# Sixty-four bytes of padding ahead of each pool that holds a token sum

## The chip, the core and the metric

The kernel runs on one core of a Trainium2 chip. The metric is the device time of one execution in microseconds (us); a shorter time is better. Several executions are timed, and their median stands for a kernel.

## The reference

One inference step of a small streaming encoder: 1024 new frames ("prompt") and 8 streams of 16 frames ("sample", 128 rows), a model width of 1024, two layers. Each layer is attention followed by an MLP with a hidden width of 4096:

```python
def mlp(x, g_norm, w_up, w_down):
    return jnp.square(jax.nn.relu(rmsnorm(x, g_norm) @ w_up)) @ w_down
...
    for layer in range(DEPTH):
        ...                      # attention; hp (prompt), hs (sample) updated
        hp = hp + mlp(hp, g_mlp[layer], w_up[layer], w_down[layer])
        hs = hs + mlp(hs, g_mlp[layer], w_up[layer], w_down[layer])
```

Everything is float32. This study is about the first MLP product, `rmsnorm(x) @ w_up`, and the change-over from it to the second.

## The kernel before, in words

A layer goes through four stages: `attention`, `wo_phase` (output projection, norm, transposes), `mlp_up` (first MLP product, relu, square) and `mlp_down` (second product).

**Arithmetic.** A float32 operand is split into a rounded part and a remainder (`split`, L106: ScalarE's CAST writes the rounded part at L109, VectorE's TENSOR_TENSOR the remainder at L115). A product of two split operands is three TensorE matmuls (`mm3`, L713: lines L715, L716 and L717). In a matmul row of the profile the names behind the arrow are the moving operand and then the stationary one, so `ps_x<-sx,w` streams 512 tokens of `sx` past 128 columns of `w`. Each matmul has its own weight load (PEld).

**mlp_up.** The product is a Strassen-like scheme with seven products instead of eight. The prompt's tokens are combined to seven "token sums", each a pair of tiles `sx` (rounded part and remainder, 8192 bytes a partition each) in a pool of its own, `h0` to `h6`; `h7` holds the sample's tokens `x8` (two tiles of 4096 bytes). `up_pools` (L727) opens these eight pools on the right side of the on-chip memory (SBUF) in the order 6, 2, 3, 5, 7, 4, 1, 0; the right side grows downwards, so each later pool lies lower. Below them come `uq` (the weight tiles `wq` of the upper half) and `ur` (three buffers `ru` for raw weights). The other weight tiles `w` and the activations `hc`, `hs` are on the left side.

The hidden width is walked in 16 blocks. A block is the seven products of 12 matmuls each, in the order X0, Z1, X5, then the sample (24 matmuls with 256 moving columns, `ps_s`), X6, Y4, the sample's two transposes (`turn`, L807), X3, Y2. The letter is the PSUM bank (`ps_x`, `ps_y`, `ps_z`), the number the product; product p streams token sum SIDE[p], which is sums 0, 1, 4, (sample), 5, 3, 2, 6 in this order. X and Y are added to, so between two products on a bank its content must be read out:

```python
product(X, 6, False, True)
a = nc.scalar.copy(v[3], X)          # L843
product(Y, 4, True, True)
b = tt(v[3], Y, v[3], ALU.add)       # L845
act(v[3], v[3])                      # L788, L789
product(X, 3, False, True)
act(v[2], X)
product(Y, 2, False, True)
tt(v[1], Y, v[1], ALU.add)           # L854
```

Block 0 is done in two halves of 256 tokens; the other fifteen stream all 512.

**mlp_down.** Its tiles are placed over those of `mlp_up`. On the right, `w2` lies where `h2` was, `s2` where `h3` was, `r5` and `r6` where `h5`, `h8` where `h7`, `s1` where `h4`, `w1` where `h1`, `s0` where `h0`. On the left, `r0` and then the residual tiles `x` follow each other upwards over the last activations, `ur` and `uq`. Before the change the borders of the two layouts coincide. The first product of `mlp_down` needs `w0` (split of `r0`) and `s0`; the second needs `w1` (split of `r1`) and `s1`.

**What sets the order.** One queue per engine, in the order in which a scheduler (a timeline simulation at build time) laid the instructions. A DMA issued by SyncE (SP) waits, in its queue, until the tiles whose place it overwrites have been read; everything behind it on SP waits with it. The first loads of `mlp_down` (`load`, L937, shown at line L938) are chained in program order and given a raised priority.

Of the kernel before, what the change touches and what calls it, by code (L numbers as in the profile page):

```python
# [75 lines left out]
class Build:  # L76
# [650 lines left out]
    def up_pools(self, st, layer):  # L727
        sx = [None] * 8
        for p in (6, 2, 3, 5, 7, 4, 1, 0):
            pool = self.pool(st, f"h{p}_{layer}", side="right")  # L730
            shape = [P, KC, P] if p == 7 else [P, 4, NT // 2 * P]
            sx[p] = [pool.tile(shape, F32R, tag=f"sx{v}", name="sx") for v in range(2)]
        qp = self.pool(st, f"uq{layer}", side="right")
        rp = self.pool(st, f"ur{layer}", side="right")
        return sx[:7], sx[7], (qp, rp)
# [1063 lines left out]
```

## Time and profile before

| what | value |
|---|---|
| median of 3 runs | 2407.91 us (2406.41 to 2412.36) |
| span of the profiled execution | 2399.3 us, 8.6 us under that median |
| TensorE busy | 2320.4 us, 97% of the span |
| ScalarE / VectorE busy | 1217.9 us (51%) / 1626.3 us (68%) |
| DMA moved | 385.88 MB, 161 GB/s in the mean |

The profile tells of one execution; its time is known by its span alone. A busy TensorE is not one at its peak: matmuls overlap, so what a matmul costs in a dense stretch is the distance from its start to the next one's start, not its listed length.

### The profile page before, as it was taken

How to read it: one execution, taken by the hardware profiler on the slowest of the kernel's cores; microseconds unless marked ns; L12 is line 12 of the kernel's file. 1: busy time of each engine (PE TensorE's matmuls, PEld its weight loads, DVE VectorE, ACT ScalarE, POOL GpSimd, SP SyncE). 2: the span in 40 equal slices, each digit the busy share in tenths (PEclk: the TensorE clock that was granted, in tenths of full speed). 3: DMA queues.
4: the chain of work that ended last, by engine and by line, in shares of the span. 5: the costliest groups of instructions: out<-in, count | busy, mean ns of one | idle time of the engine just before them, and what ended most of it. 6: DMA issues, size and time to landing. Idle time of an engine off the chain costs nothing.

```text
span 2399.3 us, 33421 instructions
## 1 busy us (share of the span) xinstructions
PE 2320.4 (97%) x11621; PEld 1935.5 (81%) x11621; DVE 1626.3 (68%) x3002; ACT 1217.9 (51%) x2423; POOL 535.6 (22%) x828
## 2 busy tenths in 40 slices
PE   7998999899999999999999999998999999999999
PEld 6786877788888888888777788887888888888887
DVE  6687786755655777776567877877655555776674
ACT  4676675555555433232267666665655555333321
POOL 3343332312112100000333434344211211000000
PEclk9998999999999999999999999999999999999999
DMA  7345546244433874342743555555434435744332
GB/s 244 122 127 168 171 156 200 95 155 158 145 128 141 323 245 146 117 141 99 237 149 111 188 161 173 173 169 174 138 127 145 154 137 200 278 140 158 112 116 114
DMA packets 218457, 385.88 MB, mean 161 GB/s; under 512 B 50408, under 2 KB 125104, under 8 KB 211120
## 3 DMA queue, kind: packets, MB, share of 16 engines
q1 hardware_dynamic: 195136, 307.16, 39.0%
q0 software_dynamic: 21776, 71.84, 7.7%
q10 hardware_dynamic: 1376, 4.74, 0.5%
q8 instruction: 92, 1.51, 0.3%
q14 instruction: 77, 0.63, 0.1%
HBM read 246.47 MB, written 136.14 MB: 159 GB/s over the span
## 4 chain that ended last, share of the span: by engine, by line
PE 82%; DMA 7%; DVE 5%; ACT 2%; issue 2%; POOL 1%; SPq 1%; ACTq 0%; DVEq 0%; POOLq 0%
PE ps_x L715 9%; PE ps_x L717 9%; PE ps_x L716 9%; PE ps_y L717 7%; PE ps_y L716 7%; PE ps_y L715 7%; PE ps_mm L186 3%; PE ps_mm L188 3%; PE ps_mm L187 3%; PE ps_tr L293 2%; PE ps_mm L147 2%; PE ps_mm L149 2%; PE ps_mm L148 2%; PE ps_s L717 1%; PE ps_s L716 1%
## 5 line engine op out<-in xcount | busy, mean ns | idle before, releaser
L109 ACT CAST w<-r 128x2048 fp32r<-128x2048 f32 x56 | 107.1, 1913 | 322.9 <-PE ps_y L717 212.1
L715 PE MATMUL ps_x<-w,s 128*128 128x512 f32 x512 | 199.5, 390 | 2.7 <-DVE hc L854 2.1
L717 PE MATMUL ps_x<-w,s 128*128 128x512 f32 x512 | 199.4, 389 | 0.0
L716 PE MATMUL ps_x<-w,s 128*128 128x512 f32 x512 | 199.2, 389 | 0.0
L186 PE MATMUL ps_mm<-w,hh 128*128 128x512 f32 x432 | 175.0, 407 | 13.8 <-ACT kw L253 5.1
L188 PE MATMUL ps_mm<-w,hl 128*128 128x512 f32 x432 | 174.3, 403 | 1.7 <-DMA hl<-hTd 1.4
L187 PE MATMUL ps_mm<-w,hh 128*128 128x512 f32 x432 | 172.5, 400 | 0.7 <-DVE w L159 0.7
L109 ACT CAST s<-s 128x2048 fp32r<-128x2048 f32 x56 | 107.1, 1913 | 117.9 <-DMA s<-hd 108.6
L115 DVE TENSOR_TENSOR w<-r,w 128x2048 fp32r<-128x2048 f32 x56 | 128.2, 2290 | 51.9 <-ACT w L109 51.9
L715 PE MATMUL ps_x<-sx,w 128*128 128x512 f32 (+1 forms) x408 | 157.8, 387 | 4.6 <-ACT hc L834 2.7
L1021 DVE TENSOR_TENSOR x<-ps_y,x 128x512 f32<-128x512 f32 x136 | 92.3, 687 | 101.1 <-PE ps_y L717 101.0
L717 PE MATMUL ps_x<-sx,w 128*128 128x512 f32 (+1 forms) x408 | 154.1, 378 | 0.0
L716 PE MATMUL ps_x<-sx,w 128*128 128x512 f32 (+1 forms) x408 | 154.1, 378 | 0.0
L109 ACT CAST w<-ru 128x512 fp32r<-128x512 f32 (+1 forms) x160 | 110.0, 708 | 85.3 <-PE ps_y L716 32.0
L717 PE MATMUL ps_y<-w,s 128*128 128x512 f32 x384 | 149.5, 389 | 0.0
L716 PE MATMUL ps_y<-w,s 128*128 128x512 f32 x384 | 149.4, 389 | 0.0
L715 PE MATMUL ps_y<-w,s 128*128 128x512 f32 x384 | 149.4, 389 | 0.0
L115 DVE TENSOR_TENSOR s<-s 128x2048 fp32r<-128x2048 f32 x56 | 128.1, 2287 | 26.5 <-ACT s L109 26.5
L115 DVE TENSOR_TENSOR ptl<-ps_tr,pth 128x512 fp32r<-128x512 f32 x180 | 122.6, 685 | 24.8 <-ACT pth L109 19.0
L115 DVE TENSOR_TENSOR w<-ru,w 128x512 fp32r<-128x512 f32 (+1 forms) x160 | 126.6, 793 | 10.9 <-ACT w L109 10.8
L109 ACT CAST pth<-ps_tr 128x512 fp32r<-128x512 f32 x180 | 104.8, 594 | 47.9 <-PE ps_tr L293 39.3
L115 DVE TENSOR_TENSOR wq<-ru,wq 128x1024 fp32r<-128x1024 f32 x32 | 39.7, 1240 | 131.9 <-ACT wq L109 131.9
(280 smaller groups left out, 6573.3 us busy)
## 6 DMA issues: line engine op xcount, KB each, us to landing
s<-hd SPq DMA_DIRECT2D x56, 1024.0 KB, 4.7
ru<-in_w_up SPq DMA_DIRECT2D x64, 512.0 KB, 3.9
r<-in_w_down SPq DMA_DIRECT2D x32, 1024.0 KB, 5.7
hd<-hc POOLq DMA_DIRECT2D x128, 256.0 KB, 2.7
hd<-hs POOLq DMA_DIRECT2D x96, 256.0 KB, 2.5
x<-xd SPq DMA_DIRECT2D x41, 512.0 KB, 4.6
o<-oTd SPq DMA_DIRECT2D x52, 256.0 KB, 4.1
hTd<-hh SPq DMA_DIRECT2D x36, 256.0 KB, 4.5
```

The source lines that it names most:

```text
L109: a = nc.scalar.copy(hi, src)
L115: return a, e.tensor_tensor(lo, src, hi.bitcast(F32), ALU.subtract)
L147: nc.tensor.matmul(ps, oh[:, k, :], w[:, 0, k, nn], start=(k == 0), stop=False)
L148: nc.tensor.matmul(ps, oh[:, k, :], w[:, 1, k, nn], start=False, stop=False)
L149: nc.tensor.matmul(ps, ol[:, k, :], w[:, 0, k, nn], start=False, stop=(k == 3))
L186: nc.tensor.matmul(ps, a, w[:, 0, k, :], start=(k == 0), stop=False)
L187: nc.tensor.matmul(ps, a, w[:, 1, k, :], start=False, stop=False)
L188: nc.tensor.matmul(ps, b, w[:, 0, k, :], start=False, stop=(k == KC - 1))
L715: a = mm(ps, ah, bh, start=first, stop=False, skip_group_check=True)
L716: mm(ps, ah, bl, start=False, stop=False, skip_group_check=True)
L717: return a, mm(ps, al, bh, start=False, stop=last, skip_group_check=True)
L1021: tt(xs[t][:, N[n]], ps, xs[t][:, N[n]], ALU.add)
```

## The change

One line in `up_pools` puts a pool of 16 floats (64 bytes a partition) on the right side ahead of each of the eight pools:

```diff
     def up_pools(self, st, layer):
         sx = [None] * 8
         for p in (6, 2, 3, 5, 7, 4, 1, 0):
+            self.pad(st, f"hpad{p}_{layer}", 16, "right")
             pool = self.pool(st, f"h{p}_{layer}", side="right")
```

`pad` (L103) opens a pool with one tile that nothing writes or reads. The pads add up from the top, so each pool moves down by another 64 bytes. Before, the first byte of every `sx`, `x8`, `w` and `wq` tile is 64 past a multiple of 512 bytes within its partition. After, by the allocation:

| pool | h6 | h2 | h3 | h5 | h7 (x8) | h4 | h1 | h0 | uq, ur |
|---|---|---|---|---|---|---|---|---|---|
| moved down by, bytes | 64 | 128 | 192 | 256 | 320 | 384 | 448 | 512 | 512 |
| distance to `w` modulo 512 | 64 | 128 | 192 | 256 | 320 | 384 | 448 | 0 | 0 |

No tile of `mlp_down` moves, so its tiles no longer coincide with those of `mlp_up`: `r0` reaches 512 bytes into `ur`, the tile `x` of token block 1 overlaps the rounded part of `wq`, `s1` the lower end of `x8`'s pool, and so on.

TensorE's instructions stand in the same order as before. SyncE's, ScalarE's and VectorE's change at the border between `mlp_up` and `mlp_down`, in the same way in both layers. (Line numbers past L730 are one higher in the changed kernel: L938 becomes L939, L843 becomes L844.)

SyncE's queue where the loads of layer 0's `mlp_down` begin, before; `ru` are raw weights of `mlp_up`, `xd` is the residual and `hd` the activations in DRAM:

```order
L743 DMA ru_8671<-in_w_up 128x4x256 [waits DMAHW6_49,DVE_49]
L938 DMA x_8945<-xd8_119 128x1024 [waits DMAHW0_49,DVE_49]
L938 DMA x_8946<-xd0_111 128x1024 [waits DMAHW7_49,DMASW0_49]
L938 DMA x_8947<-xd1_112 128x1024 [waits DMAHW1_49,DVE_49]
L938 DMA r1_8914<-in_w_down 128x4x512 [waits PE_49]
L938 DMA s0_8909<-hd0_129 128x2048 [waits DMASW3_49,PE_49]
L938 DMA s1_8901<-hd0_129 128x2048 [waits DMASW7_49,DMASW1_49,PE_49]
```

The same place in the changed kernel:

```order
L744 DMA ru_8703<-in_w_up 128x4x256 [waits DMAHW5_49,DVE_49]
L939 DMA r0_8981<-in_w_down 128x4x512 [waits DVE_49,DMAHW7_49,PE_49,Pool_49]
L939 DMA x_8985<-xd8_119 128x1024 [waits DMAHW6_49]
L939 DMA x_8986<-xd0_111 128x1024 [waits DMAHW0_49,DMASW0_49,DVE_49]
L939 DMA x_8987<-xd1_112 128x1024 [waits PE_49]
L939 DMA r1_8954<-in_w_down 128x4x512
L939 DMA s0_8949<-hd0_129 128x2048 [waits DMASW3_49]
L939 DMA s1_8941<-hd0_129 128x2048 [waits DMASW7_49,DMASW1_49,PE_49]
```

The load of `r0` stood 28 places earlier, ahead of nearly all `ru` loads, and now follows the last of them. The load of `x` for token block 1 now waits for TensorE: for the twelfth of the sample's matmuls in the last block, the last reader of `wq`'s rounded part. `r1`, `s0` and `s1` stand behind it.

ScalarE's queue in the last block of `mlp_up`, layer 0, before, from the copy ahead of the sample on; `ps_s8` and `h8` are the sample's, `h8t` is its transposed result:

```order
L839 COPY hc_8698<-ps_x_8701 128x512 [waits DMASW0_49,PE_49]
L788 ACTIVATE h8_8770<-ps_s8_8745 128x256 [waits PE_49]
L789 ACTIVATE h8_8770<-h8_8770 128x256 [waits Activation_49]
L109 CAST s0_8909<-s0_8909 128x2048 [waits DMAHW6_49]
L843 COPY hc_8700<-ps_x_8701 128x512 [waits DMASW1_49,PE_49]
L109 CAST s1_8901<-s1_8901 128x2048 [waits DMAHW7_49]
L109 CAST h8t_8818<-ps_t8_8815 128x256 [waits DMASW4_49,PE_49]
```

The same place in the changed kernel:

```order
L840 COPY hc_8730<-ps_x_8733 128x512 [waits DMASW0_49,PE_49]
L789 ACTIVATE h8_8802<-ps_s8_8777 128x256 [waits PE_49]
L790 ACTIVATE h8_8802<-h8_8802 128x256 [waits Activation_49]
L109 CAST h8t_8850<-ps_t8_8847 128x256 [waits DMASW4_49,PE_49]
L109 CAST w1_8945<-r1_8954 128x2048 [waits DMAHW5_49]
L109 CAST s0_8949<-s0_8949 128x2048 [waits DMAHW6_49]
L844 COPY hc_8732<-ps_x_8733 128x512 [waits DMASW1_49]
L109 CAST s1_8941<-s1_8941 128x2048 [waits DMAHW7_49]
```

The copy of bank X after product X6 stood behind one cast of `s0`; it now stands behind the casts of `h8t` (which waits for the sample's transposes), `w1` and `s0`. `w1`'s cast stood two places before the first row shown. On VectorE the remainders of `w1`, `s0` and `s1` and the addition of L845 stand in the same order as before, and L855 (L854 before) now follows L711 instead of preceding it.

## The prediction

> **What bounds the kernel now.** I read the page, then the busy time by stage, then the timeline around the end of `mlp_up`.
>
> ```profile
> span 2399.3 us, 33421 instructions
> ## 1 busy us (share of the span) xinstructions
> PE 2320.4 (97%) x11621; PEld 1935.5 (81%) x11621; DVE 1626.3 (68%) x3002; ACT 1217.9 (51%) x2423; POOL 535.6 (22%) x828
> ```
>
> TensorE (PE) is busy for 97% of the span. In the busy time by stretch (start and end, length, then busy time and count of PE, PEld, DVE, ACT, POOL, granted clock, DMA share, GB/s) layer 0's `mlp_up` is even fuller, and layer 1's is built alike:
>
> ```profile
> 478.00:812.00 334.00, 333.85 (x1655) 282.36 (x1653) 189.45 (x269) 186.52 (x301) 65.39 (x122) 1.00 0.46 161
> ```
>
> PE has no idle time in it that another engine could give back. So the change acts in two ways: by what a matmul costs with its streamed operand moved, and by any wait that PE meets. Both go into the time in full.
>
> What a matmul costs is read from starts in the timeline of PE (start, length, line, names); these are, in the last but one block, the first matmuls of Z1 (X5 follows it), of the sample, X6, Y4, X3 and Y2:
>
> ```profile
> 769.98 0.39 PE L715 MATMUL ps_z<-sx,w 128*128 128x512 f32 x1
> ...
> 775.42 0.28 PE L715 MATMUL ps_s<-wq,sx 128*128 128x256 f32 x1
> ...
> 778.29 0.40 PE L715 MATMUL ps_x<-sx,w 128*128 128x512 f32 x1
> ...
> 781.04 0.39 PE L715 MATMUL ps_y<-sx,w 128*128 128x512 f32 x1
> ...
> 783.90 0.48 PE L715 MATMUL ps_x<-sx,w 128*128 128x512 f32 x1
> ...
> 786.75 0.39 PE L715 MATMUL ps_y<-sx,w 128*128 128x512 f32 x1
> ```
>
> Z1 and X5 take 5.44 us for 24 matmuls: 227 ns each with 512 moving columns. The sample takes 2.87 us for 24: 120 ns with 256. So 256 more columns cost 107 ns, 512 columns cost 214, and 13 ns of every matmul, wide or narrow, are no streaming. X6, behind the sample, takes 2.75 us (229 each) and X3, behind the transposes, 2.85: after another kind of matmul the rhythm is off, and in Z1 and X5 it is back at 227. The interplay of streaming and weight load thus has a state that costs 227 and others that cost more, and all operands in these rows lie on the same residue modulo 512.
>
> **The change part by part: the cost of a matmul.** No row has a steady run with residues apart. Single pairs there are: in the sample's attention the tile `kb` has 1152 bytes, so the tiles behind it (`uks`, `pn`, `ub`) lie 128 or 256 bytes off the residue of a matmul that streams 512 columns while they are loaded as the next weights. There are 20 such pairs without another wait, between these two:
>
> ```profile
> 214.66 0.39 PE L300 MATMUL ps_pv<-pth,VS 128*128 128x512 f32 x1
> 214.88 0.33 PE L544 MATMUL ps_utr<-identr,uks 128*128 128x128 f32 x2
> ...
> 1632.69 0.39 PE L300 MATMUL ps_pv<-pth,VS 128*128 128x512 f32 x1
> 1632.92 0.33 PE L544 MATMUL ps_utr<-identr,uks 128*128 128x128 f32 x2
> ```
>
> The distances of the 20 run from 227 to 238 ns, 231.6 in the mean: none is below the steady 227, none far above it. They are the nearest rows, so I take 231.6 where residues differ: 4.9 ns more than 226.7 in Z1, X5, Y4 and Y2 (48 matmuls, 235 ns a block), and the rest up to 231.6 in X6 and X3 (2.4 ns in 12 matmuls of X6, 29 ns, and somewhat less in X3, about 50 in all). X0 keeps its residue and I give it nothing; nor do I give the sample anything (its `x8` moves by 320), whose 256-column matmuls stay at 120 ns. That is 0.285 us a block; times 15 full blocks and 2 layers, **+8.5 us**. The bounds: if residues do nothing, 0; if every one of the 2160 matmuls that move stays at 236, near the upper end of the pairs, 9.3 × 2160 = +20; if moving the residue apart freed all of the 13 ns, −28. The last has the 20 pairs against it.
>
> A rule speaks against any effect. The Trainium skill, TensorE: Matmul & The Clock Gate, section Step-by-step: what each phase is for, says that PE has two independent SBUF read ports and that "Loading the next tile's weights doesn't steal SBUF read bandwidth from the running matmul." By it this term is 0; it stands below as a rival. The uneven rhythm of X6, 229 against 227 with nothing waited for, does not fit it well.
>
> **The border between the products.** In the last block of `mlp_up` the timelines of SP, ACT, DVE and PE (in layer 0) show now:
>
> ```profile
> 783.10 2.72 SPq L938 DMA_DIRECT2D x<-xd  x3
> 789.67 0.38 SPq L938 DMA_DIRECT2D r<-in_w_down  x1
> 792.39 5.76 SPq L938 DMA_DIRECT2D s<-hd  x2
> ```
>
> ```profile
> 803.45 0.59 ACT L843 COPY hc<-ps_x 128x512 f32<-128x512 f32 x1
> 804.66 1.92 ACT L109 CAST s<-s 128x2048 fp32r<-128x2048 f32 x1 [0.62 <-DMA s<-hd]
> 806.48 0.36 ACT L109 CAST h8t<-ps_t 128x256 fp32r<-128x256 f32 x1
> ```
>
> ```profile
> 803.37 2.29 DVE L115 TENSOR_TENSOR s<-s 128x2048 fp32r<-128x2048 f32 x1 [2.72 <-ACT s L109]
> ...
> 812.17 0.68 DVE L854 TENSOR_TENSOR hc<-ps_y,hc 128x512 f32<-128x512 f32 x1
> ```
>
> ```profile
> 799.07 0.28 PE L715 MATMUL ps_s<-w,sx 128*128 128x256 f32 x1
> ...
> 805.98 0.38 PE L810 MATMUL ps_t<-identr,h 128*128 128x128 f32 x2
> 806.11 0.48 PE L715 MATMUL ps_x<-sx,w 128*128 128x512 f32 x1
> ...
> 812.91 0.50 PE L715 MATMUL ps_x<-w,s 128*128 128x512 f32 x1 [1.06 <-DVE hc L854]
> ```
>
> Now X6's copy runs at 803.45, X3 at 806.11, `mlp_down` starts at 812.91, 0.06 us after L854. With the new order: the third `x` waits for the sample's first half, which ends with the `wq` matmuls at 799.1, so it goes over 13 us later than now (783.10 + 2.72) and holds `r1`, `s0` and `s1` behind it. From 799.1 to `s0` there are 0.5 + 1 + 1 MB to bring.
>
> ```profile
> 800.00:805.00 5.00, 5.00 (x26) 4.24 (x25) 2.28 (x2) 3.53 (x5) 0.00 (x0) 1.00 1.02 373
> ```
>
> ```profile
> s<-hd SPq DMA_DIRECT2D x56, 1024.0 KB, 4.7
> ```
>
> At the 373 GB/s of this stretch 2.5 MB take 6.7 us; a 1 MB load of `s` takes 4.7 in the median from issue to landing, of which some 2.0 are not throughput (4.7 less 1 MB at 373 GB/s). `r1` lands at about 805.1, `s0` at 807.8. Then ACT, in its order: `h8t` behind the transposes, 806.4 to 806.8; `w1`, 1.9 us, to 808.7; `s0`, 1.9, to 810.6; only then X6's copy, 0.6, to 811.2. X3 needs bank X empty and starts at 811.2 instead of 806.1: **5.1 us of idle PE**, of which the DMAs set nothing as long as `s0` lands before 808.7. DVE: `w1`'s remainder (2.3 us) to 811.0, `s0`'s to 813.3, L846 (0.7) to 814.0, as X3 ends (2.85 us) at 814.1; Y2 ends at 816.8. ACT meanwhile casts `s1`, then does relu and square of v[3] from 814.0 and of X3's result (four steps at about 0.6, like the copy) to 816.5; DVE does L708, L709, L711 and L855, 0.68 each, from 816.5 to 819.2. `mlp_down` starts there instead of at 812.9: **+6.3 us**. Its own loads come some 7 us later than now, as the PE does, so I see no further stall behind it; `s0`'s lateness beyond 808.7 would add one for one.
>
> A PE that idles that long also loses clock. The idle time of 3.13 us before this row is followed by the stretch below it, at a granted clock of 0.61:
>
> ```profile
> 1208.90 1.20 PE L179 MATMUL ps_n<-identr,x 128*128 128x128 f32 x8 [3.13 <-DMA x<-xd]
> ```
>
> ```profile
> 1209.00:1212.50 3.50, 3.50 (x21) 3.50 (x22) 0.99 (x8) 2.95 (x9) 1.47 (x4) 0.61 0.39 103
> ```
>
> That is up to 1.4 us of lost matmul time; part of it falls into the wait for L855, so I add 0.9 (0 to 1.4). The Trainium skill's page of the same title, section What's actually happening, has a window of 3.4 us and half the clock after an idle one; the row agrees. A border costs 7.2 us (6.3 to 9, with `s0` up to 1.3 late), two of them **+14.4 us**. Before, PE waited 1.06 us at this place; nothing here could turn into a gain.
>
> Costed at nothing: the pads' own tiles (nothing touches them); `r0`'s later load (its place is free once the last block's weights are split, before that block starts, and `w0` is needed only behind the border); the two swapped DMA issues on POOL (`hd` is read a stage later). If that cover were gone, the border would wait for `w0` one for one.
>
> **The sum.** On the profiled execution 2399.3 + 8.5 + 14.4 = 2422.2 us of span; the timed runs are 8.6 longer at the median, which I carry over: 2407.9 + 22.9 = 2430.8, say **2431** (its own range 2424 to 2438).
>
> **The rivals.**
> - *Residues don't matter* (the two-port rule): only the borders, 2407.9 + 14.4 = 2422. For it: all of the kernel's matmuls have one residue, so no row proves an effect, and products with different tiles of the same residue all run at 227. Against it: 231.6 in the single pairs. Chance 0.33.
> - *Residues apart cost more than a broken rhythm*: each of 2160 at 236 or above, 2407.9 + 20 + 14.4 = 2442 or more. For it: single pairs lie there. Against it: the pairs' mean. 0.13.
> - *Faster*: the 13 ns are a collision of the two reads on equal residues, and pads that part them take it away: −28 + 14.4, 2394. It decides from where a matmul gains over 10 ns (21.6 / 2160), since the borders must be paid first. For it: 13 ns at both widths, as if each weight load took it. Against it: none of 20 pairs came below 227. 0.07.
> - *The change does nothing measurable*: the borders' wait is absorbed, or a small gain per matmul pays for it: about 2409. Against it: the copy's place behind two casts is fixed in ACT's queue. 0.07.
> - My forecast: 0.40.
>
> A measurement here can tell 0.3%, 7.2 us, from no change: faster is below 2400.7, slower above 2415.1. So faster 0.07, same 0.08 (the fourth rival and the fringe of the second and third), slower 0.85. The range 2416 to 2444 holds the forecast, the first rival and half of the costlier one.
>
> **What would show it.** In the changed profile: X3's first matmul in both last blocks behind an idle time of about 5 us ended by ACT L844; `mlp_down`'s first behind L855; a granted clock below 1 after it. Starts in Z1, X5, Y4 and Y2 at 230 to 233 ns. I am wrong on the borders if PE's idle there stays near 1 us, and on the matmuls if those starts stay at 227, or fall towards 214.

## The result and the profile after

The changed kernel takes 2426.69 us in the median (2422.14 to 2429.56), the kernel before 2407.16 us (2405.53 to 2412.36) beside it: the medians are 19.5 us apart. The ratio on record is 1.0094, 95% interval 1.0074 to 1.0114, which is 22.6 us of 2407.16 (17.8 to 27.4); it is not the quotient of these two medians, which is 1.0081. A second set of runs, told below, gave 1.0102 (1.0086 to 1.0117). Forecast were 2431 us, 1.0095 times the 2407.9 that the forecast started from.

The head of the page of the changed kernel's profile:

```profile
span 2427.8 us, 33429 instructions
## 1 busy us (share of the span) xinstructions
PE 2335.3 (96%) x11621; PEld 1939.2 (80%) x11621; DVE 1626.2 (67%) x3002; ACT 1218.4 (50%) x2423; POOL 537.2 (22%) x828
```

PE is busy for 15 us longer with the same 11621 instructions; the other engines do what they did. And two groups of instructions in the same page (busy time, mean ns of one, then the idle time ahead of them and what ended it):

```profile
L715 PE MATMUL ps_x<-w,s 128*128 128x512 f32 x512 | 199.4, 389 | 2.4 <-DVE hc L855 2.4
...
L715 PE MATMUL ps_x<-sx,w 128*128 128x512 f32 (+1 forms) x408 | 161.0, 395 | 14.0 <-ACT hc L844 9.4
```

Of the idle time ahead of bank X's products 9.4 us end with ScalarE's copy L844, twice 4.7: the two borders. The starts in the timeline of PE, in layer 0's last but one block, the one shown of before; these are the first matmuls of Z1, the sample, X6, Y4, X3 and Y2:

```profile
778.35 0.40 PE L715 MATMUL ps_z<-sx,w 128*128 128x512 f32 x1
...
783.91 0.28 PE L715 MATMUL ps_s<-wq,sx 128*128 128x256 f32 x1
...
786.73 0.40 PE L715 MATMUL ps_x<-sx,w 128*128 128x512 f32 x1
...
789.52 0.40 PE L715 MATMUL ps_y<-sx,w 128*128 128x512 f32 x1
...
792.42 0.48 PE L715 MATMUL ps_x<-sx,w 128*128 128x512 f32 x1
...
795.30 0.39 PE L715 MATMUL ps_y<-sx,w 128*128 128x512 f32 x1
```

Z1 and X5 now take 5.56 us (5.44 before), the sample 2.82 (2.87), X6 2.79 (2.75), Y4 with the transposes 2.90 (2.86), X3 2.88 (2.85). Nothing waits in there; the matmuls follow each other at another rhythm. In the last block, PE from the transposes on (the rows of X3, Y2 and `mlp_down`'s first product), and ScalarE beside it:

```profile
814.79 0.38 PE L811 MATMUL ps_t<-identr,h 128*128 128x128 f32 x2
819.96 0.79 PE L715 MATMUL ps_x<-sx,w 128*128 128x512 f32 x1 [4.79 <-ACT hc L844]
...
825.01 0.39 PE L715 MATMUL ps_y<-sx,w 128*128 128x512 f32 x1
...
829.18 0.50 PE L715 MATMUL ps_x<-w,s 128*128 128x512 f32 x1 [1.22 <-DVE hc L855]
```

```profile
815.21 0.37 ACT L109 CAST h8t<-ps_t 128x256 fp32r<-128x256 f32 x1 [4.93 <-PE ps_t L811]
815.48 1.90 ACT L109 CAST w<-r 128x2048 fp32r<-128x2048 f32 x1
817.52 1.90 ACT L109 CAST s<-s 128x2048 fp32r<-128x2048 f32 x1
819.32 0.58 ACT L844 COPY hc<-ps_x 128x512 f32<-128x512 f32 x1
```

ScalarE stands idle for 4.93 us because `h8t` at the head of its queue waits for the transposes; then `h8t`, `w1` and `s0` go ahead of the copy that would let X3 start. X3 then takes 5.05 us instead of 2.88. The busy time in that stretch (PE, PEld, DVE, ACT, POOL, granted clock, DMA share, GB/s):

```profile
819.90:825.10 5.20, 5.14 (x13) 4.08 (x14) 4.80 (x3) 3.16 (x4) 0.54 (x1) 0.54 1.04 414
```

The granted clock is 0.54: after the 4.79 us without work PE runs at about half speed.

The table gives, for every kernel of this study, a full block (one start of X0 to the next, the median of 28), the time from the start of the last transposes to `mlp_down`'s first matmul in layers 0 and 1, and the ratio to the kernel before, where it was timed. Kernels that ran once have none.

| kernel | block, us | last transposes to `mlp_down`, us | ratio (95%) |
|---|---|---|---|
| before | 22.21 | 6.93 / 6.93 | 1 |
| changed | 22.51 | 14.39 / 14.24 | 1.0094 (1.0074 to 1.0114) |
| changed again (e9) | 22.51 | 14.88 / 14.40 | 1.0102 (1.0086 to 1.0117) |
| e1 one pad of 512 | 22.21 | 15.15 / 14.42 | 1.0082 (1.0051 to 1.0114) |
| e2 all 64 apart | 22.65 | 14.67 / 14.42 | |
| e3 all tiles 64 higher | 22.19 | 6.91 / 7.06 | |
| e4 odd multiples of 32 | 22.63 | 13.54 / 13.99 | |
| e5 x1 later | 22.51 | 13.95 / 13.93 | |
| e6 copy free | 22.51 | 7.75 / 7.75 | |
| e7 border mended | 22.51 | 7.65 / 7.65 | 1.0033 (1.0015 to 1.0052) |
| e8 two pads of 256 | 22.21 | 15.04 / 13.54 | |
| e10 pad 512, mended | 22.21 | 7.69 / 7.68 | 1.0002 (0.9990 to 1.0015) |
| e11 sample 32 apart, mended | 22.15 | 7.68 / 7.68 | 0.9999 (0.9983 to 1.0014) |
| e12 order alone | 22.21 | 12.94 / 11.77 | 1.0049 (1.0032 to 1.0065) |

### The profile page after: what moved, and what is told of

Its sections match the earlier page's. It is cut to its first block, busy times and chain, and to the rows that moved or that the text cites. A ratio compares the mean times of both kernels' runs of the same rounds, so it can differ in the third digit from the quotient of the medians.

```text
span 2427.8 us, 33429 instructions
## 1 busy us (share of the span) xinstructions
PE 2335.3 (96%) x11621; PEld 1939.2 (80%) x11621; DVE 1626.2 (67%) x3002; ACT 1218.4 (50%) x2423; POOL 537.2 (22%) x828
## 4 chain that ended last, share of the span: by engine, by line
PE 83%; DVE 6%; DMA 6%; ACT 3%; issue 2%; POOL 1%; SPq 0%; ACTq 0%; DVEq 0%; POOLq 0%
PE ps_x L715 10%; PE ps_x L717 9%; PE ps_x L716 9%; PE ps_y L715 7%; PE ps_y L717 7%; PE ps_y L716 7%; PE ps_mm L188 3%; PE ps_mm L186 3%; PE ps_mm L187 3%; PE ps_tr L293 2%; PE ps_mm L147 2%; PE ps_mm L149 2%; PE ps_mm L148 2%; PE ps_s L716 1%; PE ps_s L715 1%
## 5 line engine op out<-in xcount | busy, mean ns | idle before, releaser
L717 PE MATMUL ps_x<-w,s 128*128 128x512 f32 x512 | 199.4, 389 | 0.0
L715 PE MATMUL ps_x<-sx,w 128*128 128x512 f32 (+1 forms) x408 | 161.0, 395 | 14.0 <-ACT hc L844 9.4
L1022 DVE TENSOR_TENSOR x<-ps_y,x 128x512 f32<-128x512 f32 x136 | 92.3, 687 | 106.1 <-PE ps_y L717 106.1
L115 DVE TENSOR_TENSOR w<-r,w 128x2048 fp32r<-128x2048 f32 x56 | 128.2, 2289 | 46.5 <-ACT w L109 46.5
L716 PE MATMUL ps_x<-sx,w 128*128 128x512 f32 (+1 forms) x408 | 157.1, 385 | 0.0
L717 PE MATMUL ps_x<-sx,w 128*128 128x512 f32 (+1 forms) x408 | 157.1, 385 | 0.0
L717 PE MATMUL ps_y<-w,s 128*128 128x512 f32 x384 | 149.4, 389 | 0.0
L115 DVE TENSOR_TENSOR s<-s 128x2048 fp32r<-128x2048 f32 x56 | 128.0, 2286 | 25.3 <-ACT s L109 23.5
L115 DVE TENSOR_TENSOR ptl<-ps_tr,pth 128x512 fp32r<-128x512 f32 x180 | 122.6, 685 | 23.9 <-ACT pth L109 18.5
L115 DVE TENSOR_TENSOR w<-ru,w 128x512 fp32r<-128x512 f32 (+1 forms) x160 | 126.6, 793 | 11.2 <-ACT w L109 11.2
L115 DVE TENSOR_TENSOR wq<-ru,wq 128x1024 fp32r<-128x1024 f32 x32 | 39.7, 1240 | 133.8 <-ACT wq L109 133.8
```

The lines of the kernel that those rows point to most:

```text
L115: return a, e.tensor_tensor(lo, src, hi.bitcast(F32), ALU.subtract)
L715: a = mm(ps, ah, bh, start=first, stop=False, skip_group_check=True)
L716: mm(ps, ah, bl, start=False, stop=False, skip_group_check=True)
L717: return a, mm(ps, al, bh, start=False, stop=last, skip_group_check=True)
L1022: tt(xs[t][:, N[n]], ps, xs[t][:, N[n]], ALU.add)
```

## The experiments: the cost of a block

**e1.** One pad of 512 bytes in place of eight of 64:

```diff
-            self.pad(st, f"hpad{p}_{layer}", 16, "right")
+            n = {6: 128}.get(p, 0)
+            if n:
+                self.pad(st, f"hpad{p}_{layer}", n, "right")
```

> All token sums, wq and ru lie 512 bytes lower, by one pad ahead of the first pool: no operand changes its residue, and the instructions at the border stand as in the changed kernel. If residues set the cost of a block (my theory), the 15 blocks between layer 0's first and last transposes take 330.6 us as before the change (335.1 after it), and only the border stays, 14.4 us from the last transposes to mlp_down against 6.9: about 2426.7 less 2 x 4.4 = 2418 us. If blocks became longer because the tiles were moved at all (late loads, another spacing of the engines' accesses), they stay at 335 us and the time at 2427. If the border belongs to the residues, it falls back to 6.9 us and the time to 2407.

Two successive transposes in the timeline of PE, a block apart:

```profile
698.70 0.38 PE L813 MATMUL ps_t<-identr,h 128*128 128x128 f32 x2
...
720.92 0.38 PE L813 MATMUL ps_t<-identr,h 128*128 128x128 f32 x2
```

22.22 us: the blocks are those of before, with the same pattern of starts, though every sum has moved. So moving costs nothing; the residues did. The border stays, and in layer 0 it is a little worse than in the changed kernel, for a reason that ScalarE's rows show:

```profile
810.85 1.90 ACT L109 CAST w<-r 128x2048 fp32r<-128x2048 f32 x1 [0.29 <-DMA r<-in_w_down]
813.34 1.90 ACT L109 CAST s<-s 128x2048 fp32r<-128x2048 f32 x1 [0.59 <-DMA s<-hd]
```

Here `r1` and `s0` come too late by 0.9 us together. The time, 2424.98 us at a ratio of 1.0082, lies above my 2418: I had subtracted the blocks from a difference of 19.5 us that was itself at the low end of its interval. The interval here, 12 to 27 us over the kernel before, holds the 16 us that the trace adds up to (15.7 for the borders, 0.4 for the blocks); by its time alone e1 can't be told from the changed kernel, and it is the blocks in the trace that part the two.

**e2.** All sums, and the sample's tokens, 64 bytes from `w`; `wq` back on its residue:

```diff
-            self.pad(st, f"hpad{p}_{layer}", 16, "right")
+            n = {6: 16}.get(p, 0)
...
+        self.pad(st, f"hpadq_{layer}", 112, "right")
         qp = self.pool(st, f"uq{layer}", side="right")
```

> All seven sums and the sample's tokens lie 64 bytes off the weights w, wq has its residue of before, same border order as the changed kernel. Theory: the residue alone sets the rhythm of a product, so all of them run like Y2 of the changed kernel (64 off, 2.794 us for 12 matmuls, 233 ns each): a full block near 22.6 us (22.21 before, 22.51 changed). Rival: what costs is the change of residue from one product to the next, so that the rhythm is never found; then a common residue lets it settle and a block is back at 22.2 us.

```profile
697.07 0.38 PE L814 MATMUL ps_t<-identr,h 128*128 128x128 f32 x2
...
719.72 0.38 PE L814 MATMUL ps_t<-identr,h 128*128 128x128 f32 x2
```

22.65 us: no settling. Six of the seven products take 2.800 to 2.803 us, 233 ns a matmul, and the distances in X0 go (ns):

```
236 231 235 231 236 231 236 231 235 231 236 231
```

Two values by turns, for as long as the residues differ. The rival, a cost of the change from one residue to the next, is out. The sample gains: 2.824 us for 24 matmuls, 117.7 ns each against 119.7. Block 0's products, which stream 256 tokens of the sums, agree: 120.0 ns a matmul in the kernel before, 117.7 to 117.8 here, and 113 to 114 in the two behind the sample (products behind a wait or behind the transposes left aside). The time was 2425.15 us in a single run.

**e3.** The kernel before with a pad of 16 floats at the left edge, above the constants, which stay where they were, and 16 floats less at the right edge:

```diff
+            self.pad(top, "base", 16)
-            self.pad(top, "edge", 104, "right")
+            self.pad(top, "edge", 88, "right")
```

> The kernel before with every tile of SBUF 64 bytes higher, weights and token sums alike; instructions in the same order. Theory (only the distance between streamed operand and weights counts): full blocks of 22.21 us and 2407 us. Rival (a tile's own position modulo 512 counts, and the old one was a lucky one): blocks of 22.4 us or more and a time of 2413 us or more.

Measured: 2401.07 us in a single run, blocks of 22.19, X0, Z1, X5 and Y2 at 2.720 us each. The 0.02 us less are in X3, 2.833 against 2.854; it follows the transposes, which stream a constant (`identr`), the one operand here that changed its distance to the others. A tile's own place does not count; the distance between the streamed tile and the weights does.

**e4.** Pads of 8, 16, 16, 16, 16, 16, 16 and 16 floats, and 8 ahead of `uq`, so that the pools lie 32, 96, 160, 224, 288, 352, 416 and 480 bytes lower.

> Sums at odd multiples of 32 bytes from the weights: X0 and Y4 at 32 and 96 or 160 and 224 modulo 256 and so on, all eight pools. Theory: residues apart cost, whatever they are: products of 2.76 to 2.83 us, block 22.4 to 22.7 us. Rival: a step below 64 bytes lets the two reads fall between each other, and a product of 12 matmuls comes in below the 2.720 us of equal residues (at best 12 x 213 ns = 2.56 us); then a faster kernel can be made of it.

Measured: 22.63 us a block, products of 2.797 to 2.810 us and X3 2.887, the sample 2.803. No residue of this kind brings the mean of a wide product below 227 ns; the lowest is 233. The time was 2432.99 us in a single run.

**e8.** Two pads of 64 floats, ahead of h6 and h4.

> Pads of 256 bytes ahead of the first pool and ahead of h4: sums 6, 2, 3, 5 and the sample's tokens lie 256 bytes off the weights modulo 512, sums 4, 1, 0 none; border order as in the changed kernel. If the rhythm goes by the residue modulo 256 (X6 of the changed kernel, 256 off, settles at 227 like equal residues do; products 64 and 192, 128 and 384 apart behave in pairs), a full block takes 22.21 us and the kernel equals e1, 2425 us. If it goes by 512, X6, Y4, X3 and Y2 stay at 2.77 to 2.88 us and the block at 22.4 us.

```profile
691.85 0.38 PE L813 MATMUL ps_t<-identr,h 128*128 128x128 f32 x2
...
714.06 0.38 PE L813 MATMUL ps_t<-identr,h 128*128 128x128 f32 x2
```

22.21 us, every product as before the change, though four sums lie 256 bytes off. The rhythm goes by the distance modulo 256 bytes, not 512. (The time of this single run, 2412.89 us, is lower than e1's because its attention stages happened to be shorter: layer 1's `mlp_up` begins 1673.8 us after the start here and at 1687.8 in e1, with borders of 15.04 and 13.54 us as long as e1's.)

## The experiments: the border

**e5.** The load of `x` for token block 1 moved behind `s1` and `h8`:

```diff
-                    load_x(ST, 0, 1)
+                    load_x(ST, 0)
...
-                load_x(2, 3)
+                load_x(1, 2, 3)
```

> The changed kernel with the load of x for token block 1 moved behind s1 and h8 in SP's queue, so that r1 and s0 no longer stand behind its wait. ScalarE's order stays as in the changed kernel: h8t, w1, s0, then the copy of bank X. Theory (ScalarE's order prices the border, the loads would have come in time): r1 and s0 land some 10 us earlier and nothing is gained, X3 still starts 5 us after the transposes, mlp_down 14.3 us after them, 2425 us. Rival (the late loads price it): X3 at 0.1 us, mlp_down at 6.9 us, about 2412 us.

SP's issues of `r1` and `s0`, and PE's start of X3:

```profile
797.30 0.38 SPq L939 DMA_DIRECT2D r<-in_w_down  x1
802.83 0.32 SPq L939 DMA_DIRECT2D s<-hd  x1
```

```profile
818.73 0.79 PE L715 MATMUL ps_x<-sx,w 128*128 128x512 f32 x1 [4.54 <-ACT hc L844]
```

The last transposes of this run start at 813.81. `r1` goes 16.5 us ahead of them and has landed 6 us before them, `s0` is issued 11 us ahead; in the changed kernel they went 6.4 and 5.9 us ahead. The wait of 4.79 us has become 4.54. The late load of `x` was there, as forecast, and it was not what cost: the rows of e1 give what it added there, 0.9 us. The time was 2424.84 us in a single run.

**e6.** What ties the copy to `s0` is written in the kernel, where `mlp_down` splits its first operands; I had read this order as the scheduler's own choice:

```diff
                 sv = ssplit(0)
-                if s == 0:
-                    self.behind(self.cut[0], self.marks[1])
-                    self.behind(self.cut[1], self.marks[2])
```

`marks[1]` is the copy of bank X, `marks[2]` the addition to it, `cut` the two halves of `s0`'s split.

> The changed kernel without the two added orders that put the copy of bank X and the addition to it behind the split of s0; the scheduler then lays the copy ahead of h8t's cast, and the splits of w1 and s0 behind it, with x1's load where the change has it. Theory: X3 starts 0.1 us after the transposes as before the change, but s0's remainder on VectorE now comes behind L855, L709 and L711, so mlp_down starts 10 us after the transposes (6.9 before, 14.3 changed): the wait goes over to mlp_down's first matmul, and 4.3 us a layer are won, about 2418 us. Rival (the copy's place is all): 6.9 us and 2412 us.

The last transposes start at 811.34, X3 0.13 us behind them. Then `mlp_down`'s first product:

```profile
819.09 0.47 PE L715 MATMUL ps_x<-w,s 128*128 128x512 f32 x1 [1.78 <-DVE hc L855]
...
822.40 0.79 PE L717 MATMUL ps_x<-w,s 128*128 128x512 f32 x1 [2.61 <-DVE s L115]
```

The wait has gone over to `mlp_down`, as expected, though not to its first matmul but to the first L717, whose wait ends with the remainder of `s0` (DVE L115). Its end is not free either: `mlp_down` takes 364.8 us in layer 0 (352.3 in the changed kernel), with a wait of 4.41 us for VectorE (L1022) some 87 us into it, and 353.0 (348.1) in layer 1. In layer 0 all of the 12.5 us more are at these two places: 7.0 are the waits, and behind each the granted clock is 0.50 (from 822.4 to 826.0 and from 910.7 to 915.0), where the changed kernel has 1.00 at the same matmuls. From `mlp_up`'s first matmul to `mlp_down`'s last product layer 0 takes 742.2 us (736.1 changed), layer 1 731.0 (734.1). So the 4.3 us a layer that I expected were not won; the time was 2428.74 us in a single run.

**e7.** e5, and `h8t`'s cast tied behind `s0`'s:

```diff
-                self.split(h8t[:, 0], h8t[:, 1], t8)
+                self.marks.append(self.split(h8t[:, 0], h8t[:, 1], t8)[0])
...
                     self.behind(self.cut[0], self.marks[1])
+                    self.behind(self.cut[0], self.marks[3])
```

> The changed kernel, all pads kept, with x1's load later as in e5 and one more added order: h8t's cast behind s0's, so that ScalarE has w1, s0, copy, h8t as before the change. Theory: the border costs 6.9 us from transposes to mlp_down as before the change, the blocks stay at 22.51 us, and what is left is their 4.4 us a layer: 2407 + 9 = 2416 us, 0.4% above the kernel before. If the residues' term is no real loss (made up by something later), the time equals that of before; if the border is made by more than ScalarE's order, mlp_down starts at 9 us or later.

ScalarE, then PE at the border; the last transposes start at 809.43:

```profile
806.62 1.90 ACT L109 CAST s<-s 128x2048 fp32r<-128x2048 f32 x1
808.42 0.57 ACT L844 COPY hc<-ps_x 128x512 f32<-128x512 f32 x1
809.84 0.37 ACT L109 CAST h8t<-ps_t 128x256 fp32r<-128x256 f32 x1 [0.85 <-PE ps_t L811]
```

```profile
817.08 0.50 PE L715 MATMUL ps_x<-w,s 128*128 128x512 f32 x1 [1.68 <-DVE hc L855]
```

The copy ends before the transposes, X3 follows them 0.13 us later, and 6.7 of the 7.4 us of a border are gone; the remaining 0.7 are one step on VectorE, as L855 still follows L711. With the blocks as in the changed kernel it takes 0.33% (0.15 to 0.52) more than the kernel before, 7.9 us (3.6 to 12.5); the traces have 8.7 for the blocks and 1.4 for what is left of the borders.

**e10.** e7 with e1's single pad in place of the eight.

> e1's single pad of 512 bytes (no residue changed) with e7's border (x1's load later, h8t's cast behind s0's). Theory: blocks 22.21 us, 7 to 7.7 us from the transposes to mlp_down; both terms gone, the time within 2 us of the kernel before. If anything besides residues and the order at the border costs, it stays 4 us or more above.

2406.76 us, ratio 1.0002: both terms are gone, and with them the whole loss (0.9990 to 1.0015).

**e12.** The kernel before, without any pad, with one order added:

```diff
-                self.split(h8t[:, 0], h8t[:, 1], t8)
+                self.marks.append(self.split(h8t[:, 0], h8t[:, 1], t8)[0])
...
                     self.behind(self.cut[0], self.marks[1])
+                    self.behind(self.marks[3], self.cut[0])
```

> The kernel before, no pad, every tile in its place; one added order puts s0's cast behind h8t's on ScalarE, and so the copy of bank X behind both. w1 and s1 are cast earlier here, so one cast less stands ahead of the copy than in the changed kernel. Theory (ScalarE's order alone makes the border's wait): X3 starts 4.79 - 2.04 = 2.8 us after the transposes, mlp_down 10 to 11 us after them against 6.9: 3 to 4 us a layer, 2 x 3.5 = 7 us over the kernel before. Rival (the moved tiles make it): no wait ahead of X3, time unchanged.

ScalarE around the transposes (start 808.76), and X3:

```profile
807.95 1.90 ACT L109 CAST s<-s 128x2048 fp32r<-128x2048 f32 x1 [3.63 <-DMA s<-hd]
809.76 0.36 ACT L109 CAST h8t<-ps_t 128x256 fp32r<-128x256 f32 x1
810.02 1.90 ACT L109 CAST s<-s 128x2048 fp32r<-128x2048 f32 x1
811.82 0.59 ACT L843 COPY hc<-ps_x 128x512 f32<-128x512 f32 x1
```

```profile
812.46 0.80 PE L715 MATMUL ps_x<-sx,w 128*128 128x512 f32 x1 [3.32 <-ACT hc L843]
```

X3 starts 3.70 us after the transposes, not 2.8: the first cast, of `s1`, waits for its load and keeps ScalarE until 809.85. The X3 of this run takes 5.29 us, at a granted clock of 0.50, so that 12.94 and 11.77 us pass until `mlp_down`, 6.0 and 4.8 more than before; I had left that clock out of the estimate. The kernel takes 0.49% (0.32 to 0.65) more, 11.8 us. The order on ScalarE makes a border of this kind with every tile in its old place.

**e9.** The changed kernel again, in more runs.

> The changed kernel once more, so that it stands beside the others on one chip. If its cost is blocks plus borders as the traces add them up (2 x 4.4 and 2 x 7.4, with nothing behind them): 23.6 us over the kernel before, ratio 1.0098. If something else in the kernel gives part of it back, the ratio stays nearer to 1.008.

2429.55 us against 2404.12, ratio 1.0102: 24.5 us (20.7 to 28.1). The traces' sum of 23.6 stands; nothing is given back.

**e11.** e10's kernel with 32 bytes of the 512 ahead of the sample's pool and 480 behind it, ahead of h4.

> As e10, but 32 bytes of the 512 ahead of the sample's pool and the rest behind it: only the sample's tokens lie apart from the weights (32 bytes). In e4 the sample's 24 matmuls took 2.803 us at such a distance, against 2.873 at equal residues. If that holds here, a block is 0.07 us shorter less what X6 loses behind it (0 to 0.04 us): 22.14 to 22.18 us, 1 to 2 us in all, below what the timing can tell; the rival is that X6 gives all of it back and the block stays at 22.21 us.

The sample takes 2.798 us, X6 2.747 as before the change, X5 2.728 (2.720): a block of 22.15. From the first to the last transposes of a layer it is 329.7 and 329.6 us (e10: 330.8 and 330.6), 2.1 us in all. The timing cannot see that: 0.9999 (0.9983 to 1.0014). Its blocks are the shortest here (e3's 22.19 comes next), and no kernel of this study is measurably faster than the kernel before.

## Why the prediction was right, and where it was not

**The matmul term: +8.5 forecast.** Between the first and the last transposes the changed kernel needs 335.13 and 334.82 us in its two layers, before 330.67 and 330.58: +8.7 us. That residues apart cost was right; the number came out in good part by luck. Z1, X5, Y4 and Y2 were to lose 235 ns a block and lost 43, 73, 44 and 74 = 234. X6 and X3 were to lose 50 and lost 36 and 25 = 61. "X0 keeps its residue and I give it nothing" is the step that failed: X0 lost 42 ns, though its sum moved by 512 and is at equal residues. Its distances (ns) in a block of the changed kernel show why:

```
229 229 233 236 224 231 236 228 233 231 226 227
```

From the third on that is, within 1 ns, the sequence of X3 behind the transposes before the change (234 235 225 230 236 229 232 231 227 226): X0 begins with the broken rhythm that Y2 leaves and takes its twelve matmuls to find 227 again. Before, Y2 left it in order. X6 has the right sign for the wrong reason: its sum lies 256 bytes off, which e8 shows to be no distance at all, and behind the sample, which lies 64 bytes off modulo 256, it goes from its third matmul on exactly as X0 does (240 238, then 233 236 224 231 236 228 233 231 226 227). The sample was given nothing either and gained 46 ns. The misses in X0 and in the sample cancel.

The price of 231.6 ns is near the products' means, 232.8 at 64 and at 128 bytes modulo 256 (Y2, X5) and 230.2 to 230.6 at 192 (Z1, Y4), but the 20 single pairs did not show it. The trace of before has 50 pairs without another wait in the same stages, from L301 to the transposes of L293, whose next weights `p` lie, by the allocation, on the residue of all the others. Two of them:

```profile
89.53 0.39 PE L301 MATMUL ps_pv<-ptl,VS 128*128 128x512 f32 x1
89.76 0.60 PE L293 MATMUL ps_tr<-identr,p 128*128 128x128 f32 x4
...
1638.23 0.40 PE L301 MATMUL ps_pv<-ptl,VS 128*128 128x512 f32 x1
1638.46 0.60 PE L293 MATMUL ps_tr<-identr,p 128*128 128x128 f32 x4
```

Their distances run from 229 to 238 ns, 232.7 in the mean: as long as in the 20 pairs, with no residue apart. So the 231.6 told nothing of residues and was no evidence against the rival by which they don't matter; that it came so near is luck. The first steady runs with residues apart are those of the changed kernel and of e2.

**The border term: +7.2 a layer.** It measured 7.46 and 7.31. The steps: X3's idle time 5.1 forecast, 4.79 and 4.59 found, ended by L844 as said; `mlp_down` behind L855, as said. "I add 0.9" for the lost clock was too small, against bounds of 0 to 1.4: X3 alone lost 2.2 us in layer 0 (5.05 against 2.85). That it did not show in the sum is due to another miss: I let VectorE's L708 to L711 and L855 run after Y2's end, 2.4 us; with X3 and Y2 so late two of the four ran before it, and `mlp_down` followed Y2 by 1.4 us. The claim that "the DMAs set nothing as long as `s0` lands before 808.7" held in the changed kernel's profile (`s0` landed 0.02 us before its cast) and failed by 0.9 to 1.1 us in layer 0 of e1 and e9: the cover had no thickness. `r0`, costed at nothing, landed 17.6 us ahead of the last transposes and held nothing up.

**The 8.6 us carried over.** I carried them over as if every execution had them on top of its span. An execution has 1.8 us of that (2429.56 us with a span of 2427.8); the rest was the spread of the executions. 28 runs of the kernel before went from 2393.03 to 2411.75 us, and in the traces it sits in the attention stages: `mlp_up` begins 435.4 to 445.3 us after the start. Since forecast and result were both set against medians, it did no harm.

**The rivals.** Residues without effect (2422 us): out by e1 against the changed kernel, and by e7. Faster by parted reads: out by e2 and e4 for 512 columns. "236 or above" for all: out, the means were 230 to 233 in the products at another distance. The rule that a weight load does not take bandwidth from the running matmul (the Trainium skill, TensorE: Matmul & The Clock Gate, Step-by-step: what each phase is for) would make residues indifferent; the runs differ from that by up to 3%: the same matmuls take 227 or 233 ns by nothing but the distance of their two operands.

**What stays open.** Which weights the distance counts against, those in use or those being loaded, was not told apart, as both always have one residue here. Why equal residues settle is not known; the runs show only that they do. And which overlap made the scheduler lay `h8t` and `w1` ahead of `s0` is not settled: not `x`'s load, since e5 has that order too. The other overlaps, `r0` over `ur` and `s1` over the sample's pool among them, were not tried one by one.

## What to carry to other kernels

A change of layout is two changes: what the addresses do to the instructions, and what the new overlaps do to the order in which they are laid; read the second from the queues at every change-over of tiles, where it was here the larger part (14.8 of 23.5 us). A hand-set order that says "copy behind cast" is safe only as long as the cast is early; when its neighbours move it turns into a wait, and e6 shows that taking it away may only pass the wait on. Price a wait of PE with the clock that follows it: here 4.8 us of waiting cost 2.2 more. And before a price is taken from the nearest rows, look for rows like them in which the supposed cause is missing: here those had the same price.

## What the runs showed of the hardware

- A matmul that streams 512 columns starts every 226.7 ns when streamed operand and weights lie at equal addresses modulo 256 bytes, at both addresses tried (e3) and 256 or 512 bytes apart as well (e8, e1); 230 to 234 ns in a product's mean at the other distances tried, in a fixed pattern (e2: 231 and 236 by turns).
- With 256 columns it is the other way round: 119.7 ns at equal residues, 117.7 at 64 bytes (e2) and 116.6 at 32 bytes (e11).
- A rhythm broken by transposes, by matmuls of another width or by a product at another distance takes up to twelve matmuls to settle at equal residues, and so costs the product that follows as well (X0 behind Y2: 42 ns).
